# High and low halves of the stationary rows stored side by side in the output projection and layer 1

## The chip, the cores and the metric

The kernel runs on one core of one Trainium2 chip, as one launch. The metric is device time in microseconds, from the first to the last of the kernel's work on that core. Two runs of the kernel before gave 1775.3 and 1775.44 us, median 1775.37 us.

## The reference, cut to what matters

A two-layer backbone in float32 works on 256 latent tokens and 256 context tokens of width 2048. Layer 0 projects both streams, runs neighbourhood attention and a bidirectional state-space scan beside each other, and joins their 4096 output channels in one projection. Layer 1 is a gated short convolution between two more projections.

```python
# layer 0, after attention (ya) and the scan (yb)
out = jnp.concatenate([ya, yb], axis=-1) @ w_out          # 256x4096 @ 4096x2048
x = x + gate * out
# layer 1
h = modulate(rms_norm(x, norm_g[1]), shift, scale)
p = h @ sc_w_in                                           # 256x2048 @ 2048x8192
bg, cg, hv, g = jnp.split(p, 4, axis=-1)
y = bg * dw_conv(cg * hv, conv_w)
x = x + gate1 * ((jax.nn.silu(g) * y) @ sc_w_out)         # 256x2048 @ 2048x2048
```

## The kernel before, in words

**Products in three parts.** Each float32 operand of a large product is split into a high half, rounded to the matmul's fast float32 form (`F32R`), and a low half, the remainder. A product is then three matmuls: high times high, high times low, low times high. Weights come by DMA in pieces of 512 KB (`raw`), ScalarE writes their high half (`wH`, line 417) and VectorE their low half (`wL`, line 424). The activations are split once, where they are produced.

**Who is stationary.** `mm_act` keeps the activations stationary: for each block `kb` of 128 channels and each half `t` of the 256 tokens it loads 128 columns of the activation's high or low half into the array, and streams 512 columns of the weights through it. `mm_ws` does it the other way round, with weights stationary and 256 or 512 token columns moving. All of the output projection and of layer 1 goes through the first form, or through loops written out with the same three calls. So there the pair of halves of one activation block, a tile of 128 partitions by 2 by 256 elements, is read only as a stationary operand. Each matmul has its own weight load; the trace lists them apart, as PE (the matmul) and PEld (the load of its stationary operand). The calls all stand in one helper, line 192.

**Where the pairs of halves are made.** Four places write such a tile, always the high half on ScalarE and then the low half on VectorE: `put_mix` (line 945) and `mix_gen` (line 1562) for the 32 blocks of the output projection, `high` and `low` in `norm_gen` for the 16 blocks that enter layer 1, and `bg_gen` for the 16 blocks that enter its last projection. In the trace these tiles are named `mix`, `h` and `y`. They reuse the memory of the 32 tiles `hH0` to `hH15` and `hL0` to `hL15` of layer 0: `mix0` to `mix15` and `y` use the `hH` ones, `mix16` to `mix31` and `h` the `hL` ones. In layer 0 itself those tiles hold one half for 512 tokens each, and are read both as stationary and as moving operands.

**What sets the order.** The program is written out in one order by a planner inside the kernel. `Plan` keeps an estimated clock per engine and, per 128-element stretch of a tile, when it was last written and read; `pump` starts queued pieces of work (generators in `urgent`, `side` and `back`) between matmuls when the estimate says their inputs are ready. Three pools of scratch tiles (`tmp`, `half`, `raw`) are handed out by the same clocks, and a generator starts only when its share of `tmp` and `half` is free (`budget`). So a change in tile sizes or in a pool can move pieces of work in the order, without adding any.

Of the kernel before, what the change touches and what calls it, by code (L numbers as in the profile page):

```python
# [9 lines left out]
F32R = mybir.dt.float32r  # L10
# [21 lines left out]
for _name, _w in (("ident", 128), ("sel", 2), ("mhalf", 32), ("strip", 384), ("mask", 64)):  # L32
    _coff[_name] = (_n, _n + _w)
    _n += _w
NCONST, CFIRST = _n, 162


class Plan:
# [103 lines left out]
def kernel(ctx: ExitStack, tc, x, cx, ada0, w0, ada_w, ada_b, w_in, w_out, sc_in, sc_out, rpb, small, const,  # L142
# [3 lines left out]
    sb = ctx.enter_context(tc.tile_pool(name="sb", bufs=1))  # L146
# [6 lines left out]
    E = plan.add  # L153

    def st(shape, tag, dt=F32, name=None):
        return sb.tile(list(shape), dt, tag=tag, name=name or tag, bufs=1)

    def drt(shape, name):
        return dr.tile(list(shape), F32, name="dram_" + name)


    NTMP, NHALF, NRAW, NW = 9, 9, 5, 3
    free_t = [st([128, 512], f"tmp{k}") for k in range(NTMP)]
    free_h = [st([128, 256], f"half{k}") for k in range(NHALF)]
    free_b = [pj.tile([128, 512], F32, tag=f"bank{k}", name=f"bank{k}", bufs=1) for k in range(8)]
    free_r = [st([128, 1024], f"raw{k}") for k in range(NRAW)]
    WH = [st([128, 1024], f"wH{k}", F32R) for k in range(NW)]
    WL = [st([128, 1024], f"wL{k}", F32R) for k in range(NW)]
# [167 lines left out]
    def give(pool, *bs):  # L336
        pool.extend(bs)
# [300 lines left out]
    hH, hL = [None] * KB, [None] * KB  # L638
# [301 lines left out]
    def put_mix(i, o):  # L940
        if free_rows[0] > i % 16:

            yield W_("ACT", o)
            hl = st([128, 2, 256], f"hH{i}" if i < 16 else f"hL{i - 16}", F32R, name=f"mix{i}")
            E(S.copy(hl[:, 0], o))
            yield W_("DVE", hl[:, 0])
            E(V.tensor_tensor(out=hl[:, 1], in0=o, in1=hl[:, 0].bitcast(F32), op=ALU.subtract))
            mH[i] = hl
            give(free_h, o)
            return  # L950
        yield W_("AQ", o)
        E(DMA2.dma_start(mixd[i], o))
        give(free_h, o)
        written.add(i)
# [79 lines left out]
    def head_gen(a, h):  # L1034
# [89 lines left out]
        give(free_b, po)  # L1124
        attn[0] += 2
        yield from put_mix(hd, o)


# [242 lines left out]
    def group_gen(s, gi):  # L1371
# [104 lines left out]
        for b in range(2):  # L1476
            yield from put_mix(16 + 2 * g + b, ys[b])
# [70 lines left out]
    def mix_gen(ip):  # L1548
        pair = (2 * ip, 2 * ip + 1)
        yield when(lambda: all(i in written or mH[i] is not None for i in pair) and free_rows[0] > (2 * ip + 1) % 16)  # L1550
        pair = [i for i in pair if mH[i] is None]
        if not pair:
            return
        i0, n = pair[0], len(pair)
        yield W_("AQ", mixd[i0:i0 + n])
        mx = tmp()
        m3 = two(mx)
        E(DMA2.dma_start(m3[:, :n], mixd[i0:i0 + n].rearrange("b p c -> p b c")))
        yield W_("ACT", mx)
        for j, i in enumerate(pair):  # L1560
            hl = st([128, 2, 256], f"hH{i}" if i < 16 else f"hL{i - 16}", F32R, name=f"mix{i}")
            E(S.copy(hl[:, 0], m3[:, j]))
            E(V.tensor_tensor(out=hl[:, 1], in0=m3[:, j], in1=hl[:, 0].bitcast(F32), op=ALU.subtract))
            mH[i] = hl
        give(free_t, mx)

    def mixes(k):
        for ip in order[k::3]:
            yield from mix_gen(ip)
# [80 lines left out]
    def norm_gen():  # L1650
# [5 lines left out]
        hls = {}  # L1656
# [42 lines left out]

        def high(kb, tt):  # L1700
            if kb not in hls:
                hls[kb] = st([128, 2, 256], f"hL{kb}", F32R, name=f"h1_{kb}")
                h1[kb] = (hls[kb][:, 0], hls[kb][:, 1])
            E(S.activation(hls[kb][:, 0, tt], late[kb][:, tt], AF.Identity, bias=S1[:, kb:kb + 1], scale=1.0))

        def scaled(kb, tt):

            o = pts[kb // 4][:, kb % 4:kb % 4 + 2, tt]
            E(V.tensor_tensor(out=o, in0=o, in1=rb[0][:, tt].unsqueeze(1).to_broadcast([128, 2, 128]), op=ALU.mult))
            high(kb, tt)  # L1710
            high(kb + 1, tt)

        def pair(kp):
            yield when(lambda: ("turn", kp + 1) in got)
            yield W_("DVE", r2, held[kp] if kp in held else late[kp])
            for kb in (kp, kp + 1):
                if kb not in held:
                    E(V.tensor_tensor(out=late[kb], in0=late[kb], in1=r2, op=ALU.mult))
                else:
                    E(V.scalar_tensor_tensor(out=late[kb], in0=held[kb][:, (kb % 2) * 256:(kb % 2) * 256 + 256],  # L1720
                                             scalar=A1[:, kb:kb + 1], in1=r2, op0=ALU.mult, op1=ALU.mult))
                high(kb, slice(0, 256))
            if kp in held:
                give(free_b, held[kp])
            ahead()
# [52 lines left out]
    for ns in ((0, 512), (1024,), (1536,)):  # L1778
        pss = [banks(2) for n in ns]
        for ip in range(16):  # L1780
# [8 lines left out]
            if hold[0]:  # L1789
# [10 lines left out]
                for t in range(2):  # L1800
                    done_ = 0
                    for q, (H, Lo) in enumerate(ws):
                        for b in range(2):
                            i = 2 * order[NTAIL + q] + b
# [39 lines left out]
    v = st([128, 4, 256], "Btm", name="v")  # L1844
# [16 lines left out]
    def over(rows_, b):  # L1861

        yield W_("PE", *rows_, nb=1)
        pt = bank()
        for k in range(2):
            for t in range(2):
                turn(pt[:, k * 256 + t * 128:k * 256 + (t + 1) * 128], rows_[t][:, (b + k) * 128:(b + k + 1) * 128])
        return pt
# [39 lines left out]
    def bg_gen(i, ps):  # L1908
        for t in range(2):
            yield W_("DVE", ps[t])  # L1910
            E(V.tensor_tensor(out=sg[t], in0=ps[t], in1=sg[t], op=ALU.mult))
            give(free_b, ps[t])
        for b in range(0, 4, 2):
            pt = yield from over(sg, b)
            yield W_("DVE", pt)
            E(V.tensor_tensor(out=flat(v[:, b:b + 2, :]), in0=pt, in1=flat(v[:, b:b + 2, :]), op=ALU.mult))
            give(free_b, pt)
            yield W_("ACT", v[:, b:b + 2, :])
            for k in range(2):
                kb = 4 * i + b + k  # L1920
                hl = st([128, 2, 256], f"hH{kb}", F32R, name=f"y2_{kb}")
                E(S.copy(hl[:, 0], v[:, b + k, :]))
                yield W_("DVE", hl[:, 0])
                E(V.tensor_tensor(out=hl[:, 1], in0=v[:, b + k, :], in1=hl[:, 0].bitcast(F32), op=ALU.subtract))
                y2[kb] = hl

    for i in range(4):
        for part, gen in ((1, cg_gen), (2, hv_gen), (3, gg_gen), (0, bg_gen)):
            ps = banks(2)
            kb0 = 0  # L1930
            if i == 0 and part == 1:

                kb0 = 8
                ws = []
                for t in range(2):
                    for kb in range(8):
                        force(lambda: ("h1", kb, t) in got, (urgent,))
                        if kb // 2 == len(ws):
                            ws.append(use(kb // 2))
                        H, Lo = ws[kb // 2]  # L1940
                        tt = slice(t * 128, (t + 1) * 128)
                        for a_, w_ in ((0, H), (0, Lo), (1, H)):
                            mm(ps[t], h1[kb][a_][:, tt], w_[:, kb % 2], kb == 0 and a_ == 0 and w_ is H, False)
                        if t and kb % 2:
                            used()
                        pump()
            for kb in range(kb0, KB, 2):
                force(lambda: ("h1", kb + 1, 1) in got)
                chunk(kb, "act", ps, kb == 0, kb == KB - 2, lambda i: h1[i])
            spawn(urgent, ordered(4 * i + (1, 2, 3, 0).index(part), gen(i, ps)), 2 if i == 0 and part in (1, 2) else 0)  # L1950
# [30 lines left out]
    for t in range(2):  # L1981
        for q, (H, Lo) in enumerate(ws):
            for b in range(2):
                hl = y2[KB - 6 + 2 * q + b]
# [66 lines left out]
```

## Time and profile before

| what | us |
|---|---|
| two runs | 1775.3 and 1775.44 |
| the profiled execution, first to last instruction | 1770.0 |
| TensorE matmuls, busy | 1749.4 |
| weight loads, busy (they overlap matmuls) | 1472.7 |
| VectorE busy | 1262.5 |
| ScalarE busy | 773.7 |
| output projection, first to last matmul start | 1127.4 to 1318.7 |
| matmuls of layer 1's first projection | 1319.8 to 1677.1 |
| matmuls of layer 1's last projection | 1677.4 to 1765.1 |

A group in the profile is named by what it writes and reads: `bank<-wH,mix` is a matmul that streams `wH` past the stationary `mix` into a PSUM bank, and the load with the same name loads that stationary. In the timeline the columns are start, length, engine, line, operation, tiles, shape and count; lengths of matmuls overlap, because the next one starts before the last has drained, so the pace is read from one start to the next. In the table by windows each engine has its busy time and its number of instructions in brackets.

### The profile page before, as it was taken

Reading aid. Unit: us, or ns where it says so; the run is one execution under the profiler, and the core shown is the slowest. Engines: PE = TensorE matmul, PEld = TensorE weight load, DVE = VectorE, ACT = ScalarE, POOL = GpSimd, SP = SyncE. Lnnn points to the kernel's source line nnn. Section 1 sums busy time; section 2 is a strip of 40 time slices with the busy share of each in tenths; the row PEclk is TensorE's granted clock in tenths of the full one; section 3 lists DMA queues with packets and bytes.
Section 4 is the critical chain, followed back from the end, with each engine's and each line's share of the span. In section 5 each row is a group of like instructions: output and inputs, shape, how many; then the busy total and the mean of one; then the engine's idle time right before and its main releaser. Section 6 shows DMA issues by size and latency. Waiting matters only on the chain.

```text
span 1770.0 us, 25382 instructions
## 1 busy us (share of the span) xinstructions
PE 1749.4 (99%) x9577; PEld 1472.7 (83%) x9577; DVE 1262.5 (71%) x1986; ACT 773.7 (44%) x1330; POOL 31.3 (2%) x28
## 2 busy tenths in 40 slices
PE   6999999999999999999999999999999999999998
PEld 4777988888888889888888898888888888888887
DVE  5656788878686878775878777786668777555554
ACT  5423544455242445342445343564546344444442
POOL 0000100001000001000001000000000000000000
PEclk9999999999999999999999999999999999999999
DMA  9977644666746666655666556658867787666563
GB/s 362 348 284 255 208 148 142 194 203 202 232 140 200 200 195 200 207 148 185 205 191 191 160 174 213 189 184 286 284 224 242 250 259 253 207 188 190 190 211 119
DMA packets 218138, 374.60 MB, mean 212 GB/s; under 512 B 32304, under 2 KB 69008, under 8 KB 218016
## 3 DMA queue, kind: packets, MB, share of 16 engines
q1 hardware_dynamic: 210704, 366.38, 64.1%
q10 hardware_dynamic: 7312, 6.61, 1.2%
q8 instruction: 75, 1.23, 0.3%
q14 instruction: 47, 0.39, 0.1%
HBM read 367.52 MB, written 6.72 MB: 211 GB/s over the span
## 4 chain that ended last, share of the span: by engine, by line
PE 97%; DMA 1%; DVE 1%; ACT 0%; SPq 0%; issue 0%; POOL 0%; DVEq 0%; ACTq 0%
PE bank L192 94%; PE bank L196 3%; DMA tmp<-dram_csr 1%; DMA raw<-in_ada 0%; DVE wL L424 0%; DVE acc L812 0%; SPq L578 0%; DVE tmp L1405 0%; DVE tmp L1416 0%; DVE tmp L598 0%; ACT wH L417 0%; DVE acc L798 0%; DVE half L1443 0%; ACT tmp L1401 0%; ACT half L719 0%
## 5 line engine op out<-in xcount | busy, mean ns | idle before, releaser
L417 ACT CAST wH<-raw 128x1024 fp32r<-128x1024 f32 (+1 forms) x375 | 392.0, 1046 | 586.1 <-PE bank L192 493.1
L424 DVE TENSOR_TENSOR wL<-raw,wH 128x1024 fp32r<-128x1024 f32 (+1 forms) x374 | 453.4, 1215 | 219.5 <-ACT wH L417 217.9
L192 PE MATMUL bank<-hH,wH 128*128 128x256 f32 (+1 forms) x1040 | 342.9, 330 | 0.0
L192 PE MATMUL bank<-hL,wH 128*128 128x256 f32 (+1 forms) x1040 | 336.8, 324 | 0.0
L192 PE MATMUL bank<-hH,wL 128*128 128x256 f32 (+1 forms) x1024 | 331.1, 323 | 0.0
L192 PE MATMUL bank<-wH,hH 128*128 128x512 f32 x640 | 256.4, 401 | 2.6 <-ACT hH L752 2.6
L192 PE MATMUL bank<-wL,hH 128*128 128x512 f32 x640 | 250.1, 391 | 0.0
L192 PE MATMUL bank<-wH,hL 128*128 128x512 f32 x640 | 249.8, 391 | 0.1
L812 DVE SCALAR_TENSOR_TENSOR acc<-raw,csil,acc 128x512 f32<-128x512 f32 x256 | 191.7, 749 | 62.3 <-DMA raw<-in_ada_w 55.6
L192 PE MATMUL bank<-wH,h 128*128 128x512 f32 x680 | 215.7, 391 | 0.0
L192 PEld LDWEIGHTS bank<-hH,wH 128*128 128x128 f32 x1040 | 197.7, 190 | 17.0 <-issue 2.2
L192 PEld LDWEIGHTS bank<-hL,wH 128*128 128x128 f32 x1040 | 197.9, 190 | 15.0
L192 PEld LDWEIGHTS bank<-hH,wL 128*128 128x128 f32 x1024 | 194.6, 190 | 15.7 <-DVE wL L424 0.4
L192 PEld LDWEIGHTS bank<-wH,h 128*128 128x128 f32 x680 | 127.6, 188 | 26.6 <-issue 0.2
L192 PEld LDWEIGHTS bank<-wH,hH 128*128 128x128 f32 x640 | 120.6, 189 | 30.6 <-issue 4.6
L192 PEld LDWEIGHTS bank<-wH,hL 128*128 128x128 f32 x640 | 120.4, 188 | 25.5 <-DVE hL L758 0.6
L192 PEld LDWEIGHTS bank<-wL,hH 128*128 128x128 f32 x640 | 120.7, 189 | 23.9 <-DVE wL L440 0.3
L192 PE MATMUL bank<-wH,mix 128*128 128x512 f32 x432 | 137.9, 392 | 0.0
L192 PE MATMUL bank<-wL,h 128*128 128x512 f32 x340 | 132.3, 389 | 0.0
L192 PEld LDWEIGHTS bank<-wH,mix 128*128 128x128 f32 x432 | 81.1, 188 | 16.7 <-issue 0.2
L192 PE MATMUL bank<-wL,mix 128*128 128x512 f32 x216 | 84.1, 389 | 0.0
L192 PEld LDWEIGHTS bank<-wL,h 128*128 128x128 f32 x340 | 63.9, 188 | 12.9
(284 smaller groups left out, 2168.2 us busy)
## 6 DMA issues: line engine op xcount, KB each, us to landing
raw<-in_w_in SPq DMA_DIRECT2D x196, 512.0 KB, 3.9
raw<-in_ada_w SPq DMA_DIRECT2D x128, 512.0 KB, 4.7
raw<-in_sc_in SPq DMA_DIRECT2D x128, 512.0 KB, 3.7
raw<-in_w_out SPq DMA_DIRECT2D x64, 512.0 KB, 4.9
raw<-in_ada SPq DMA_DIRECT2D x36, 512.0 KB, 5.9
raw<-in_sc_out SPq DMA_DIRECT2D x32, 512.0 KB, 4.1
PT<-in_ada SPq DMA_DIRECT2D x16, 512.0 KB, 8.9
tmp<-dram_csr SPq DMA_DIRECT2D x32, 256.0 KB, 6.4
```

The source lines that it names most:

```text
L192: E(T.matmul(o, l, r, start=start, stop=stop, skip_group_check=True))
L196: E(T.transpose(o, i, ident if k == 128 else ident[:k, :k]))
L417: E(S.copy(H, v))
L424: E(V.tensor_tensor(out=Lo, in0=v, in1=H.bitcast(F32), op=ALU.subtract))
L812: E(V.scalar_tensor_tensor(out=acc, in0=v[:, j], scalar=csil[:, 2 * k + j:2 * k + j + 1], in1=acc, op0=ALU.mult, op1=ALU.add))
```

## The change

The tile of 128 by 2 by 256 elements stays as large, but element `c` of the high half now stands at place `2c` and element `c` of the low half at `2c + 1`. A half is then read and written with a step of two elements (8 bytes), where it was contiguous. This holds for `mix`, `h` and `y`. Layer 0's own use of the tiles is contiguous as before.

Besides, the tiles `hL0` to `hL3` grow from 512 to 576 elements, and the pairs stored in them begin 8, 16, 32 and 48 elements (32, 64, 128 and 192 bytes) further on. That concerns `mix16` to `mix19` and `h` blocks 0 to 3. The 1 KB per partition for it comes from the pool `half`, which has eight tiles and not nine.

```diff
+SHIFT = {"hL0": 8, "hL1": 16, "hL2": 32, "hL3": 48}

     def st(shape, tag, dt=F32, name=None):
+        if tag in SHIFT:
+            return sb.tile([128, 576], dt, tag=tag, name=name or tag, bufs=1)[:, :512]
         return sb.tile(list(shape), dt, tag=tag, name=name or tag, bufs=1)
+
+    def pair_rows(tag, name):
+
+        wide = tag in SHIFT
+        v = sb.tile([128, 576 if wide else 512], F32R, tag=tag, name=name, bufs=1)
+        o = SHIFT.get(tag, 0)
+        return v[:, o:o + 512].rearrange("p (c a) -> p a c", a=2)

-    NTMP, NHALF, NRAW, NW = 9, 9, 5, 3
+    NTMP, NHALF, NRAW, NW = 9, 8, 5, 3
...
-            hl = st([128, 2, 256], f"hH{i}" if i < 16 else f"hL{i - 16}", F32R, name=f"mix{i}")
+            hl = pair_rows(f"hH{i}" if i < 16 else f"hL{i - 16}", f"mix{i}")
             E(S.copy(hl[:, 0], o))
             yield W_("DVE", hl[:, 0])
             E(V.tensor_tensor(out=hl[:, 1], in0=o, in1=hl[:, 0].bitcast(F32), op=ALU.subtract))
...
-                hls[kb] = st([128, 2, 256], f"hL{kb}", F32R, name=f"h1_{kb}")
+                hls[kb] = pair_rows(f"hL{kb}", f"h1_{kb}")
...
-                hl = st([128, 2, 256], f"hH{kb}", F32R, name=f"y2_{kb}")
+                hl = pair_rows(f"hH{kb}", f"y2_{kb}")
```

`mix_gen` changes in the same way as `put_mix`.

More of the change, by code (lines that the diff above doesn't have):

```diff
@@ L1560, in mix_gen @@
         for j, i in enumerate(pair):
-            hl = st([128, 2, 256], f"hH{i}" if i < 16 else f"hL{i - 16}", F32R, name=f"mix{i}")
+            hl = pair_rows(f"hH{i}" if i < 16 else f"hL{i - 16}", f"mix{i}")
             E(S.copy(hl[:, 0], m3[:, j]))
```

## The prediction

> **What bounds the kernel now.** I read the page first, then the table by windows over the stages that the change touches, then the timeline for the pace of single matmuls.
>
> ```profile
> span 1770.0 us, 25382 instructions
> ...
> PE 1749.4 (99%) x9577; PEld 1472.7 (83%) x9577; DVE 1262.5 (71%) x1986; ACT 773.7 (44%) x1330; POOL 31.3 (2%) x28
> ...
> PEclk9999999999999999999999999999999999999999
> ...
> PE 97%; DMA 1%; DVE 1%; ACT 0%; SPq 0%; issue 0%; POOL 0%; DVEq 0%; ACTq 0%
> ```
>
> TensorE is the chain: 97% of what ended last, at a full clock in every slice. So a microsecond is won or lost only by the pace of the matmuls, or by a wait in front of them. The stages of the change, by windows: end of layer 0, output projection, the seam between the layers, layer 1's two projections.
>
> ```profile
> core 0: us, PE busy (x) PEld busy (x) DVE busy (x) ACT busy (x) POOL busy (x), PEclk, DMA share, GB/s
> 1080.00:1127.00 47.00, 47.00 (x232) 38.65 (x232) 27.34 (x56) 19.95 (x43) 0.00 (x0) 1.00 0.62 189
> 1127.00:1315.00 188.00, 188.00 (x903) 156.44 (x902) 137.92 (x202) 97.16 (x149) 1.39 (x2) 1.00 0.73 247
> 1315.00:1320.00 5.00, 5.00 (x28) 4.19 (x27) 3.19 (x10) 2.73 (x7) 0.56 (x1) 1.00 0.58 212
> 1320.00:1677.00 357.00, 356.99 (x1633) 294.91 (x1632) 235.21 (x286) 162.62 (x199) 0.94 (x1) 1.00 0.68 219
> 1677.00:1770.00 93.00, 88.50 (x395) 72.96 (x393) 47.61 (x52) 29.69 (x31) 0.00 (x0) 0.99 0.50 165
> ```
>
> Up to 1677 TensorE never stops; in the last stage it stops for 4.5 us. VectorE is busy for 137.92 of 188 us and 235.21 of 357 us, ScalarE for less. The instructions that touch the three rearranged tiles, with the whole span as window, in the order `mix`, `h`, `y` (columns: PE, PEld, DVE, ACT):
>
> ```profile
> 0.00:1770.00 1770.00, 178.79 (x768) 143.05 (x768) 12.17 (x32) 11.47 (x32) 1.00 0.66 212
> 0.00:1770.00 1770.00, 352.37 (x1536) 287.23 (x1536) 8.41 (x24) 8.86 (x24) 1.00 0.66 212
> 0.00:1770.00 1770.00, 87.75 (x384) 71.92 (x384) 6.21 (x16) 5.88 (x16) 1.00 0.66 212
> ```
>
> That is 768 + 1536 + 384 = 2688 matmuls whose stationary operand is now read with a step, all 512 columns wide. **One nanosecond more or less for each of them is 2.69 us.**
>
> **The pace of a matmul, and what is fixed in it.** Starts in the timeline: first 512 columns in layer 1, then 256 columns in layer 0, then attention's products with the halves of V, also 256 columns.
>
> ```profile
> 1559.71 1.75 PE L192 MATMUL bank<-KL,h 128*128 128x512 f32 x7
> 1561.30 0.39 PE L192 MATMUL bank<-QT,h 128*128 128x512 f32 x1
> ```
>
> ```profile
> 205.75 0.28 PE L192 MATMUL bank<-hH,wH 128*128 128x256 f32 x1
> ...
> 207.55 0.28 PE L192 MATMUL bank<-hH,wH 128*128 128x256 f32 x1
> ```
>
> ```profile
> 278.04 0.28 PE L192 MATMUL bank<-PH,VH 128*128 128x256 f32 x1
> ...
> 279.44 0.40 PE L192 MATMUL bank<-KT,QT 128*128 128x512 f32 x1
> ```
>
> Seven starts in 1.59 us are 227 ns each (over long steady stretches of the trace, 226.7); fifteen in 1.80 us are 120.0; twelve in 1.40 us are 116.7. From 256 to 512 columns the pace grows by 106.7 ns, 0.417 ns a column. So 226.7 − 512 × 0.417 = 13.3 ns are left that do not depend on the width. This rest comes once with each load of 128 stationary columns. It is not merely a price of swapping operands: V's halves lie 32 bytes off the 512-byte raster on which the program's addresses place all other operands of these matmuls, and with them the rest is 116.7 − 106.7 = 10.0 ns. So where the stationary lies in memory changes the rest, and I read it as time that the moving stream loses while the stationary is fetched.
>
> **The change part by part.** *The load itself.* It has room, as its length, its start and a narrower load show:
>
> ```profile
> L192 PEld LDWEIGHTS bank<-wH,h 128*128 128x128 f32 x680 | 127.6, 188 | 26.6 <-issue 0.2
> ...
> L192 PEld LDWEIGHTS bank<-tmp,xtm 128*64 128x64 f32 x128 | 7.2, 136 | 4.2 <-issue 1.8 <-DVE tmp L1421 1.6 <-DVE tmp L1416 0.7
> ```
>
> ```profile
> 1500.16 0.19 PEld L192 LDWEIGHTS bank<-wL,h 128*128 128x128 f32 x1
> 1500.38 0.39 PE L192 MATMUL bank<-wL,h 128*128 128x512 f32 x1
> ```
>
> ```profile
> 206.23 0.19 PEld L192 LDWEIGHTS bank<-hH,wL 128*128 128x128 f32 x1
> ...
> 206.35 0.28 PE L192 MATMUL bank<-hH,wL 128*128 128x256 f32 x1
> ```
>
> From 64 to 128 columns a load grows by 52 ns, so of the 188 ns some 104 scale with the columns. In layer 1 its matmul starts 220 ns after it, some 30 ns after its end; in layer 0, 120 ns after it, before its end. A load whose scaling part doubled would let its matmul go at 120 + 104 = 224 ns, still inside 226.7: nothing. If the matmul waited for the longer load's end and the same 30 to 36 ns after it, it would start at 188 + 104 + 36 = 328 ns: 101 ns × 2688 = +272 us. I take the lower end, since layer 0 shows matmuls that do not wait for the end.
>
> *The rest of 13.3 ns.* No row shows a stationary with a step. A load now spans 1024 bytes of each partition instead of 512. Lower bound: all of the rest goes, −13.3 × 2688 = −35.8 us; nearest row below, V's 10.0 ns: −9 us. Upper bound: it is paid per stretch of memory fetched, of which there are twice as many: +13.3 ns, a pace of 240, +35.8 us. I take the upper end: the one row that moves the rest at all ties it to where the stationary is fetched, and twice as much memory is walked through in the same load.
>
> [...]
>
> *The four shifted tiles.* `mix16` to `mix19` serve 4 × 24 matmuls and `h` 0 to 3 serve 4 × 96: 480 of the 2688. By V's row a 32-byte offset is worth −3.3 ns, −1.6 us if all four had it; with the opposite sign +1.6. I take 0.
>
> *Writing with a step.* VectorE writes the low halves in 12.17 + 8.41 + 6.21 = 26.8 us, ScalarE the high ones in 11.47 + 8.86 + 5.88 = 26.2 us. No row shows such a write. Unchanged is one bound (a gain is excluded, a scattered write is no less work), doubled the other: +27 us on each engine. TensorE covers it, since both engines have over a quarter of each stage free. Where that cover is thin is the seam: the first blocks of `h` are awaited there, and 8 of the 24 half-block pairs in a row at 8.41 / 24 + 8.86 / 24 = 0.72 us, less their overlap, could add up to 3 us. I take 1 us.
>
> *The order.* The program built from the change has exactly the same instructions; 52 of 1237 places differ on ScalarE, 88 of 1988 on VectorE and 34 of 833 on SyncE, nearly all around the output projection, because of the smaller pool and the planner's wider stretches. The two windows up to 1315 have TensorE busy for 235 of 235 us, so work moved between matmuls only trades places. 0, with ±2 us.
>
> Sum: 1770.0 + 35.8 + 1 = 1806.8 us for the profiled span; the 5.4 us by which the median of the runs (1775.37) exceeds this span stay. **Forecast: 1812 us**, 2.1% slower; its own range is 1790 (half of the step is paid) to 1850 (the load's doubling shows as well).
>
> **Rivals.** *Nothing happens* (1776 us): the load is hidden by its slack and the rest stays 13.3 ns. For it: 226.7 and 120.0 are 17 and 9 times 13.3, as if starts were held to a raster, where a small extra cost vanishes. Against it: V's 116.7 is on no such raster.
>
> *Faster: the two streams stop disturbing each other.* The moving operand passes 4 bytes per 0.417 ns; a contiguous load of 104 ns passes 512 bytes, half as fast, so the streams drift past each other all through it. With a step of 8 bytes the load passes 1024 bytes in 104 ns, as fast as the moving one. Streams in step can miss each other for good. If half of the rest goes, the time is 1775.4 − 17.9 = 1757 us, at V's rest 1766, at most 1740. For it: V's row says that relative position matters. Against it: nothing in the trace shows the rest below 10 ns at full streaming pace. It decides if the pace of `h` falls below 226 ns.
>
> *The load becomes the bound*: up to 1775 + 272 = 2047 us, if the stepped load takes over 300 ns. Against it is the slack above.
>
> **How the numbers follow.** Forecast 0.42, nothing 0.24, faster 0.20, load the bound 0.14. The range of 8 in 10 goes from 1755 (most of faster) to 1870 (forecast with a partly longer load) and leaves out the far end of the load and the last of faster. Two per cent, about what a measurement of this kernel can tell from no change, is 35.5 us, so slower begins at 1811 and faster below 1740. Slower has all of the load's case and about 0.3 of the forecast's, 0.45; faster has the extreme of its rival, 0.03; the rest, 0.52, is within.
>
> **What would show it.** The pace of `bank<-wH,h` in the timeline decides: near 240 ns the forecast, 227 nothing, 213 to 223 faster, far over 240 the load, whose length (188 ns now) would then show it. The pace at blocks 0 to 3 of `h` beside the other blocks shows what the shift does. Layer 0 must stay at 227 and 120 ns; if the time moves there, or TensorE stops between 1315 and 1320, my sum has left out a wait.

## The result, and the profile after

| | us | ratio to the kernel before, 95% interval |
|---|---|---|
| before, median of 2 runs | 1775.37 | |
| after, median of 2 runs (1790.53 and 1792.55) | 1791.54 | 1.0097 [1.008, 1.0114] |

The change makes the kernel slower by 16.2 us, 0.97%. The forecast was 1812 us: the direction is right, the size is more than twice too large. The page of the changed kernel:

```profile
span 1788.4 us, 25384 instructions
...
PE 1766.5 (99%) x9577; PEld 1488.8 (83%) x9577; DVE 1263.4 (71%) x1986; ACT 773.1 (43%) x1330; POOL 32.2 (2%) x28
...
PE 95%; DMA 2%; DVE 2%; ACT 1%; issue 0%; SPq 0%; POOL 0%; DVEq 0%; ACTq 0%
```

The span grew by 18.4 us and TensorE's busy time by 17.1 us, with the same 9577 matmuls. VectorE and ScalarE are as busy as they were. TensorE is still the chain, with 95% of what ended last, so the time should have gone into the pace of matmuls. Where, the table by windows tells for the instructions that touch the three rearranged tiles, in the order `mix`, `h`, `y` (columns: PE, PEld, DVE, ACT):

```profile
0.00:1788.40 1788.40, 184.00 (x768) 147.52 (x768) 12.27 (x32) 12.01 (x32) 1.00 0.65 209
0.00:1788.40 1788.40, 361.47 (x1536) 296.26 (x1536) 8.42 (x24) 9.03 (x24) 1.00 0.65 209
0.00:1788.40 1788.40, 91.10 (x384) 75.30 (x384) 6.31 (x16) 6.26 (x16) 1.00 0.65 209
```

Against before, TensorE is busy for 5.21, 9.10 and 3.35 us more: 17.66 us together, nearly all that the span gained. The pace is read best where one moving tile is used twelve times in a row: from the start of that row to the start of the next are twelve matmuls. The timeline of before, and then of after, in layer 1's first projection:

```profile
1340.18 2.88 PE L192 MATMUL bank<-KL,h 128*128 128x512 f32 x12
1342.90 0.39 PE L192 MATMUL bank<-QT,h 128*128 128x512 f32 x1
```

```profile
1570.51 2.96 PE L203 MATMUL bank<-KL,h 128*128 128x512 f32 x12
1573.31 0.39 PE L203 MATMUL bank<-QT,h 128*128 128x512 f32 x1
...
1741.36 2.99 PE L203 MATMUL bank<-KL,y 128*128 128x512 f32 x12
1744.19 0.40 PE L203 MATMUL bank<-QT,y 128*128 128x512 f32 x1
```

Before, 2.72 us for twelve, 226.7 ns each. After, 2.80 us, 233.3 ns each, and 2.83 us, 235.8 ns, at `y`. So a matmul with a stepped stationary costs 6.67 ns more, not 13.3. Layer 0 has kept its pace; fourteen starts in 1.68 us are still 120.0 ns:

```profile
205.32 0.28 PE L203 MATMUL bank<-hH,wH 128*128 128x256 f32 x1
...
207.00 0.28 PE L203 MATMUL bank<-hH,wL 128*128 128x256 f32 x1
```

The groups of single tiles (minimum, median and maximum of the length in ns, then first and last start) show the load after, and the writes of ScalarE and VectorE, first contiguous (before, lines 1562 and 1563) and then stepped (after):

```profile
L203 PEld LDWEIGHTS bank<-wH,h x680: 192/193/198, 1325.7 to 1689.2; 128*128 128x128 f32 x170
```

```profile
L1562 ACT CAST mix<-tmp x24: 390/402/408, 1095.1 to 1137.0; 128x256 fp32r<-128x256 f32 x24
L1563 DVE TENSOR_TENSOR mix<-tmp,mix x24: 416/418/427, 1096.9 to 1138.6; 128x256 fp32r<-128x256 f32 x24
...
L1573 ACT CAST mix<-tmp x24: 399/418/427, 1096.0 to 1138.2; 128x256 fp32r<-128x256 f32 x24
L1574 DVE TENSOR_TENSOR mix<-tmp,mix x24: 416/418/429, 1097.9 to 1140.1; 128x256 fp32r<-128x256 f32 x24
```

The load takes 193 ns where it took 188. ScalarE's write took 402 ns before and takes 418; VectorE's is 418 ns in both.

### The profile page after: what moved, and what is told of

Same layout as the page of the kernel before. It is cut to its first block, busy times and chain, and to the rows that moved or that the text cites. A ratio compares the mean times of both kernels' runs of the same rounds, so it can differ in the third digit from the quotient of the medians.

```text
span 1788.4 us, 25384 instructions
## 1 busy us (share of the span) xinstructions
PE 1766.5 (99%) x9577; PEld 1488.8 (83%) x9577; DVE 1263.4 (71%) x1986; ACT 773.1 (43%) x1330; POOL 32.2 (2%) x28
## 4 chain that ended last, share of the span: by engine, by line
PE 95%; DMA 2%; DVE 2%; ACT 1%; issue 0%; SPq 0%; POOL 0%; DVEq 0%; ACTq 0%
PE bank L203 92%; PE bank L207 3%; DMA tmp<-dram_csr 1%; DMA raw<-in_ada 0%; DVE wL L435 0%; DVE acc L823 0%; ACT wH L428 0%; DVE tmp L1416 0%; DVE tmp L1427 0%; ACT tmp L1412 0%; SPq L589 0%; DVE half L1454 0%; DVE half L1451 0%; DVE tmp L609 0%; ACT tmp L1422 0%
## 5 line engine op out<-in xcount | busy, mean ns | idle before, releaser
L203 PE MATMUL bank<-wH,h 128*128 128x512 f32 x680 | 219.5, 395 | 0.0
L203 PEld LDWEIGHTS bank<-hH,wH 128*128 128x128 f32 x1040 | 197.8, 190 | 17.1 <-issue 2.2
L203 PEld LDWEIGHTS bank<-wH,h 128*128 128x128 f32 x680 | 131.7, 194 | 26.7 <-issue 0.4
```

The source lines that it names most:

```text
L203: E(T.matmul(o, l, r, start=start, stop=stop, skip_group_check=True))
```

## The experiments

Twelve runs, all beside runs of the kernel before on the same chip (its median 1772.69 to 1774.26 us). Single profiles of the same instructions differ by some 3 us in when layer 0 ends; the stretch from the first matmul on `mix` to the first on `y`, 550.0 us before and 564.1 us after, does not share that.

**1. The step alone.** The tiles are not enlarged or shifted and the pool `half` keeps nine tiles; the rest is the change.

```diff
-SHIFT = {"hL0": 8, "hL1": 16, "hL2": 32, "hL3": 48}
+SHIFT = {}
-    NTMP, NHALF, NRAW, NW = 9, 8, 5, 3
+    NTMP, NHALF, NRAW, NW = 9, 9, 5, 3
```

> The halves side by side, without the shift of four tiles and with all nine tiles of the pool half; TensorE's order is that of the kernel before. If the step of the stationary read is the cause, the pace of the 2688 matmuls is 233.3 ns everywhere, blocks 0 to 3 included, against 226.7 before: +6.67 x 2688 = +17.9 us, 1793 us, some 1 us more than the changed kernel, whose shifted blocks run at 229 to 234 ns. If the shift or the moved order is the cause, it is 1775 to 1777 us.

Measured: 1792.48 us, ratio 1.01 [1.0085, 1.0115]. The step by itself makes the whole loss. Its windows for `mix`, `h` and `y`:

```profile
0.00:1789.40 1789.40, 183.49 (x768) 147.31 (x768) 12.20 (x32) 11.85 (x32) 1.00 0.66 209
0.00:1789.40 1789.40, 362.15 (x1536) 295.77 (x1536) 8.46 (x24) 9.04 (x24) 1.00 0.66 209
0.00:1789.40 1789.40, 90.23 (x384) 73.98 (x384) 6.24 (x16) 6.11 (x16) 1.00 0.66 209
```

Against before, TensorE has 9.78 us more on `h` and 2.48 us more on `y`, which is 6.4 and 6.5 ns for each matmul. `y` does not show the 3.35 us of the changed kernel; the last run below comes back to that.

**2. The shift, the pool and the order alone.** Contiguous halves as before, but `hL0` to `hL3` enlarged and shifted, and `half` with eight tiles.

```diff
-        return v[:, o:o + 512].rearrange("p (c a) -> p a c", a=2)
+        return v[:, o:o + 512].rearrange("p (a c) -> p a c", a=2)
```

> The halves contiguous again, but the shift of four tiles, the smaller pool and so nearly the order of the changed kernel kept. If the step is the cause, the pace is 226.7 ns but for the 480 matmuls on shifted blocks, which may go to 223 to 235: 1773 to 1778 us. If the order or the pool costs the time, it is 1790 us.

Measured: 1777.16 us, ratio 1.002 [1.0011, 1.003]. Windows for `mix`, `h` and `y`:

```profile
0.00:1777.80 1777.80, 179.92 (x768) 143.02 (x768) 12.26 (x32) 11.58 (x32) 1.00 0.67 211
0.00:1777.80 1777.80, 354.59 (x1536) 287.37 (x1536) 8.41 (x24) 8.88 (x24) 1.00 0.67 211
0.00:1777.80 1777.80, 87.76 (x384) 71.95 (x384) 6.31 (x16) 5.97 (x16) 1.00 0.67 211
```

TensorE has 1.13 and 2.22 us more than before on `mix` and `h`, and only 96 and 384 of their matmuls read shifted pairs. On `h` that is 5.8 ns for each. The 1.13 us on `mix` would be 11.8 ns for each, so part of it has another source, the order for instance; this was not separated. From the first matmul on `mix` to the first on `y` it is 553.3 us, 3.3 more than before. So a contiguous stationary that merely lies elsewhere also costs nearly the 6.67 ns, with no more memory walked through. That spoke against the price per stretch of memory, and the next runs pursue it.

Not every other place costs something. The enlarged tiles push block 1 of `mix` and block 1 of `y`, 24 matmuls each, 256 bytes out of the old relation to the weights, by the program's addresses. Yet `y` takes 87.76 us where it took 87.75; 24 times 6.67 ns would be 0.16 us.

**3. Twice the step.** The low and high halves of both token halves interleaved, so that a half is read with a step of 16 bytes and a load walks through 2048 bytes. The writes step by 16 bytes as well. As in the first experiment no tile is shifted. One line of the edit:

```diff
+        self.v = v.rearrange("p (c t a) -> p a t c", t=2, a=2)
```

> Each stationary half read with a step of four elements (16 bytes): the halves of both token halves share one stretch, element c of half a of tokens t at place 4c + 2t + a. If the loss grows with the memory that a load walks through (512 bytes 13.3 ns, 1024 bytes 20.0 ns), 2048 bytes give 33.3 ns or more, a pace of 246.7: +20 x 2688 = +54 us, 1829 us. If any step other than one costs the same single stretch of 6.67 ns, it is 1793 us. [...]

Measured: 1808.78 us, ratio 1.0193 [1.0178, 1.0208]. The load and the pace:

```profile
L225 PEld LDWEIGHTS bank<-wH,h x680: 307/310/334, 1331.0 to 1705.5; 128*128 128x128 f32 x170
```

```profile
1358.55 2.98 PE L225 MATMUL bank<-KL,h 128*128 128x512 f32 x12
1361.37 0.39 PE L225 MATMUL bank<-QT,h 128*128 128x512 f32 x1
```

Now the load is long, 310 ns, and still the pace is 2.82 us for twelve, 235 ns: four times the memory of before, and 8.3 ns more. In a steady row, neither a price in proportion to the memory walked (226.7 + 3 × 6.67 = 246.7 ns, if the step of two elements set the scale) nor a load that bounds the pace (310 ns and more) is what happens. The matmul does go before its load has ended: the first load with `KL` starts at 1332.4 us and its matmul at 1332.6, while such a load takes 0.31 us.

The run as a whole loses more than this pace explains: 8.3 ns for 2688 matmuls are 22.3 us, and it takes 34.8 us longer than before. Twice TensorE stops and waits for weights, 4.9 us in all, and after each stop the granted clock (PEclk, the last column but two) is about half, 0.55 over 3.4 us and 0.50 over 2.4 us:

```profile
1132.00:1135.40 3.40, 3.26 (x8) 2.61 (x9) 3.40 (x8) 3.40 (x9) 0.00 (x0) 0.55 0.74 217
1355.00:1357.40 2.40, 2.40 (x7) 1.91 (x6) 2.40 (x3) 0.91 (x1) 0.00 (x0) 0.50 0.71 215
```

So the total of this run is not to be read as a price of the step; why TensorE has to wait there was not followed up.

**4 and 5. Contiguous halves, 32 or 64 bytes off the weights.** The kernel before with 8 or 16 elements of padding ahead of the tiles of layer 0's activations. Weights stay where they were, and the tiles of the activations (with `mix`, `h` and `y`) move against them. The order of the instructions is that of before on every engine. With 64 bytes one small scratch tile also shares the memory of another.

```diff
+    st([128, 8], "pad")
     xnT = [st([128, 512], ("Bl", "Cl")[kb] if kb < 2 else f"hL{kb}", name=f"xm{kb}") for kb in range(KB)]
```

> The kernel before with 32 unused bytes in front of the activation tiles, so that all stationary rows lie 32 bytes off the place that the moving weights have in a 512-byte raster, in layer 0 too; the order on every engine is that of the kernel before. If the relative place sets the loss as with V's halves before (10.0 ns, not 13.3), the pace of 4608 matmuls of 512 columns and 1920 of 256 falls by 3.3 ns: up to -22 us, 1754 us. If only the step matters, it is 1775 us. If the 235 ns seen at the one start before V's products is what a 32-byte offset costs behind 512 columns, it is +8 x 4608 = +38 us, 1813 us.

> The kernel before, contiguous rows, all activation tiles 64 bytes off. If the fetch repeats every 64 bytes, this is aligned again: 226.7 ns, 1775 us. If it repeats in a wider raster, some 233 ns for 512 columns, 1800 us; any pace below 226.7 ns would make this the fastest version.

Measured: 1799.96 us with 32 bytes, ratio 1.0149 [1.0132, 1.0166], and 1799.54 us with 64 bytes (one run). This is slower than the change itself, without any step, because layer 0's wide matmuls pay as well (by the record of starts 233.2 ns on average with 32 bytes, 227.6 before); `h` alone takes 362.04 us of TensorE with 32 bytes and 362.14 with 64, as in run 1 with the step (362.15). The timeline with 32 bytes, in layer 0, in attention's products with V and in layer 1:

```profile
205.30 0.28 PE L192 MATMUL bank<-hH,wL 128*128 128x256 f32 x1
...
206.94 0.28 PE L192 MATMUL bank<-hL,wH 128*128 128x256 f32 x1
...
280.21 0.28 PE L192 MATMUL bank<-PL,VH 128*128 128x256 f32 x1
...
281.53 0.40 PE L192 MATMUL bank<-KT,QT 128*128 128x512 f32 x1
...
1354.88 2.96 PE L192 MATMUL bank<-KL,h 128*128 128x512 f32 x12
1357.68 0.40 PE L192 MATMUL bank<-QT,h 128*128 128x512 f32 x1
```

With 512 columns 2.80 us for twelve, 233.3 ns, the pace of the changed kernel. With 256 columns fourteen starts in 1.64 us, 117.1 ns, which is less than the 120.0 of before. So the row of attention's products with V on which the prediction leaned (256 columns, 32 bytes off, 116.7 ns) is confirmed, but its sign turns round at 512 columns. V itself shows the same from the other side: by the program's addresses this padding cancels its 32 bytes, and its products go at 120.0 ns here (eleven starts in 1.32 us), where they went at 116.7.

**6 and 7. Step and offset together.** The first experiment with the same padding of 32 and 64 bytes, one run each.

> Side by side, and all activation tiles 32 bytes off the raster of the moving weights (layer 0, contiguous, too). For the 2688 stepped matmuls: if the loss is set by how much memory a load walks through, the pace is 233.3 ns as without the offset. If it is set by where the two streams stand to each other, it changes, to the 229 to 231 ns that the short runs on the block shifted by 32 bytes had in the changed kernel, or lower. The rest of the kernel is as in the run of contiguous rows 32 bytes off (233.3 ns for 512 columns, 118.6 for 256): some 1800 us if the stepped ones stay at 233, 1788 at 229.

> The same with 64 bytes. By memory walked through 233.3 ns for the stepped matmuls; by place 230 to 236, as the short runs on the block shifted by 64 bytes had. Contiguous rows of layer 0: 226.7 if the raster is of 64 bytes, 233 if it is wider.

Measured: 1797.25 and 1789.60 us. The stepped matmuls with 64 bytes:

```profile
1351.44 2.92 PE L203 MATMUL bank<-KL,h 128*128 128x512 f32 x12
1354.20 0.39 PE L203 MATMUL bank<-QT,h 128*128 128x512 f32 x1
```

2.76 us for twelve, 230.0 ns. With 32 bytes TensorE has 14.11 us more than before on the three tiles, 5.2 ns for each matmul, so that the pace lies between the two values expected. The two prices do not add up: with 64 bytes of offset a stepped stationary is faster (230.0) than a contiguous one (233.3, run 5) and faster than a stepped one without offset (233.3).

**8. Fewer places.** The kernel before, with other reads of the stationary in layer 1: in its first projection all 128 columns are the same element (no memory is walked through), in its last the step is three elements. Both projections then multiply with other activations than the reference's.

```diff
+        if name.startswith("y2_"):
+            l = bass.AP(tensor=l.tensor, offset=l.offset // 128, ap=[[512, 128], [3, 128]])
+        elif name.startswith("h1_"):
+            l = l[:, :1].to_broadcast([128, 128])
```

> The kernel before, but what the stationary operand reads is changed and with it the result: in layer 1's first projection all 128 columns read one and the same place (4 bytes per partition), in its last projection they read the tile with a step of three elements (12 bytes). If the loss is proportional to the memory walked through, the first projection's pace falls to 213 ns (-13 x 1536 = -20 us for that stage). If the 13.3 ns are a fixed raster of two stretches of 6.67 ns, it stays at 226.7, or loses one stretch, 220. [...]

Measured: 1784.02 us (one run). The window of `h`, then the pace in both projections and the loads:

```profile
0.00:1782.10 1782.10, 358.16 (x1536) 288.17 (x1536) 8.39 (x24) 8.87 (x24) 1.00 0.65 210
```

```profile
1342.91 2.91 PE L197 MATMUL bank<-KL,h 128*128 128x512 f32 x12
1345.66 0.40 PE L197 MATMUL bank<-QT,h 128*128 128x512 f32 x1
...
1701.11 2.99 PE L197 MATMUL bank<-KL,y 128*128 128x512 f32 x12
1703.94 0.39 PE L197 MATMUL bank<-QT,y 128*128 128x512 f32 x1
```

```profile
L197 PEld LDWEIGHTS bank<-wH,h x680: 185/188/192, 1322.4 to 1682.8; 128*128 128x128 f32 x170
...
L197 PEld LDWEIGHTS bank<-wH,y x168: 251/252/254, 1689.1 to 1777.0; 128*128 128x128 f32 x168
```

Reading a single element takes 2.75 us for twelve, 229 ns, and over the whole stage 358.16 us against 352.37, which is 3.8 ns more for each matmul. That is slower than the contiguous 226.7, where a price per memory walked should have given about 213. Unless reading one place over and over has a cost of its own, this rules out the forecast's reason. With the step of three elements it is 2.83 us for twelve, 235.8 ns, and a load takes 252 ns.

**9 and 10. Read or write.** Both halves of the change are separated on the 1152 matmuls of `mix` and `y`. Run 9 is the kernel before, which writes contiguously, with a stepped read; run 10 is the first experiment, which writes with a step, with a contiguous read. The edit of the helper that issues the matmuls is shown first for run 9, then for run 10. In both, the output projection and the last projection multiply with high and low halves mixed up. `h` keeps the read of the kernel that each starts from.

```diff
+        if l.tensor.name.startswith(("mix", "y2_")):
+            l = bass.AP(tensor=l.tensor, offset=l.offset // 256 + l.offset % 256 // 128 * 256, ap=[[512, 128], [2, 128]])
```

```diff
+        if l.tensor.name.startswith(("mix", "y2_")):
+            l = bass.AP(tensor=l.tensor, offset=l.offset % 2 * 256 + l.offset // 256 * 128, ap=[[512, 128], [1, 128]])
```

> The kernel before, with contiguous rows, but the matmuls of the output projection and of layer 1's last projection (tiles mix and y2, 768 + 384 = 1152 matmuls) read 128 elements with a step of 8 bytes out of the same tile; the stationary rows are then a mixture of high and low halves, so the result is not the reference's. If the step of the read is the whole cause: 233.3 ns at mix and y, 226.7 at h, 1152 x 6.67 = +7.7 us, about 1783. If the writing with a step or the changed tiles take part in it: less, down to 1775 and 226.7 ns everywhere.

> The experiment with the halves side by side in whole 512-byte tiles, but the same 1152 matmuls (tiles mix and y2) read 128 contiguous elements out of the side-by-side rows; the writes keep their step, and the result is not the reference's. If the read is the whole cause: 226.7 ns at mix and y, 233.3 at h, about 1792 - 7.7 = 1785. If writing with a step slows TensorE's reads: 233.3 ns everywhere, 1792.

Measured: 1781.54 us, ratio 1.0048 [1.0031, 1.0065], and 1784.29 us, ratio 1.006 [1.0045, 1.0075]. Windows for `mix`, `h` and `y`, of run 9 and then of run 10:

```profile
0.00:1777.70 1777.70, 183.49 (x768) 147.31 (x768) 12.17 (x32) 11.45 (x32) 1.00 0.65 211
0.00:1777.70 1777.70, 352.37 (x1536) 287.27 (x1536) 8.41 (x24) 8.87 (x24) 1.00 0.65 211
0.00:1777.70 1777.70, 91.10 (x384) 75.30 (x384) 6.21 (x16) 5.89 (x16) 1.00 0.65 211
```

```profile
0.00:1781.30 1781.30, 178.79 (x768) 143.08 (x768) 12.21 (x32) 11.81 (x32) 1.00 0.65 210
0.00:1781.30 1781.30, 362.20 (x1536) 295.57 (x1536) 8.44 (x24) 9.05 (x24) 1.00 0.65 210
0.00:1781.30 1781.30, 87.75 (x384) 71.92 (x384) 6.22 (x16) 6.14 (x16) 1.00 0.65 210
```

TensorE's times follow the read alone. With a stepped read `mix` takes 183.49 us, as in the first experiment, though written contiguously. With a contiguous read it takes 178.79 us, to the hundredth what it took before, though written with a step. ScalarE's times follow the write (11.81 against 11.45 us on `mix`), and nobody waits for that.

**11. Everything moved together.** The kernel before, with the 32 bytes of padding ahead of all tiles, so that weights and activations keep their relation.

```diff
+    st([128, 8], "pad")
     free_t = [st([128, 512], f"tmp{k}") for k in range(NTMP)]
```

> The kernel before, with every tile of the memory moved by the same 32 bytes, so that stationary and moving operand keep their relation to each other and only the place of both changes. If the relation decides: 226.7 and 120 ns and 1775, no change. If the place decides, as an alignment of each operand by itself: about 233 ns wherever 512 columns are moved, 1797 to 1800 as with half of the tiles moved, or more, as now both operands are off.

Measured: 1776.33 us, ratio 1.0011 [0.9998, 1.0023].

```profile
1560.74 2.88 PE L193 MATMUL bank<-KL,h 128*128 128x512 f32 x12
1563.46 0.39 PE L193 MATMUL bank<-QT,h 128*128 128x512 f32 x1
```

2.72 us for twelve, 226.7 ns again, and 550.0 us from `mix` to `y`, as before. By the program's addresses nearly all operands of these matmuls lie 128 bytes past a multiple of 512 before, and 160 bytes past it here. So, for contiguous rows, it is not the place of the stationary by itself that costs the 6.67 ns, but its relation to the place of the moving one: 226.7 ns with both moved by 32 bytes, 233.3 with the stationary moved alone (run 4).

**12. The changed kernel again.**

> The changed kernel once more. If the 235 to 239 ns at the last projection's high halves belong to this order of instructions and these places, they come again, and the time is 1790 to 1793; if they were of one execution, y runs at 233.3 ns there too.

Measured: 1790.98 us, and `y` takes 91.10 us of TensorE again, as in run 9, which has another order of instructions around it. So it was no chance of one execution. By the record of starts, the three kinds of matmul on `y` take 235.0, 238.3 and 233.3 ns in these runs and 233 to 234 ns in the first experiment, with the same steps and, but for one block, the same places modulo 512 bytes. Run 1 was on another chip than runs 9 and 12, so the chip is not excluded. Why a stage settles in the one pattern or the other stays open; it is worth 0.9 us.

## Why the prediction was wrong, and where it was right

**What bounds the kernel** was right: TensorE stays the chain, and 17.66 us of slower matmuls account for the 18.4 us of the span.

**The load itself, zero from a span of 0 to 272 us**: right. It takes 193 ns instead of 188, and its matmul does not wait for its end; run 3 shows even a load of 310 ns under a pace of 235. Nor are the 5 ns more of load the 6.67 ns: run 4's loads are no longer than before, 287.49 against 287.23 us on `h`, and its matmuls are as slow as the stepped ones (233.3 ns). The load's length by the step was 188 ns for contiguous rows or one element, 193 for step two, 252 for step three and 310 for step four. The pace of the matmuls does not follow it: with a step of two the load is only 5 ns longer and the matmul behind it loses 6.67 ns, and from step two to step four the load grows by 117 ns and the pace by 1.7.

**The rest of 13.3 ns doubles, +35.8 us**: this is the step that failed. The rest went from 13.3 to 20.0 ns, so it grew by half of what was forecast: 17.66 us were measured over the 2688 matmuls. The reason, "it is paid per stretch of memory fetched", was wrong, and not only its size: no memory walked through leaves 229.2 − 213.3 = 15.9 ns by run 8's twelve, 512 bytes leave 13.3 or 20.0 according to where they lie (runs 4 and 11), 1024 bytes 20.0 or 16.7 (runs 1 and 7), 2048 bytes 21.7 (run 3). The sign came out as forecast, but not for the reason given, and that much was luck.

What the runs show in its place: at 512 columns, contiguous rows in the same relation to the weights as before, or 256 bytes from it (run 2), have the least rest seen; every other offset or step that was tried costs 2.5 to 9 ns more. That a step of two elements costs this because it gives up that relation, as an offset does, is a reading: the two prices are alike (runs 1 and 4) and do not add up (runs 6 and 7), but no run shows how the one becomes the other. That it is the moving stream that loses the time while the stationary is fetched also fits and was not shown. The prediction had one row that moved the rest at all, V's, at another width; it took from it that the relative place matters, which runs 4 and 11 bear out, and then a scale, which it could not give.

**The four shifted tiles, 0 ± 1.6 us**: wrong in size when alone (+3.3 us in run 2, and 5.8 ns for each shifted matmul on `h`, where V's row had suggested 3.3 either way). In the changed kernel no loss by them can be seen: 1791.54 us, against 1792.48 without them in run 1.

**Stepped writes, hidden but for 1 us**: right in that they are hidden. ScalarE's cost 16 ns more of 402, VectorE's nothing, and run 10's `mix` and `y` run as before with them. The 1 us at the seam was not needed. Windows of after over the seam and the stage behind it:

```profile
1320.00:1326.00 6.00, 5.83 (x30) 4.62 (x30) 4.25 (x11) 2.73 (x7) 0.56 (x1) 1.00 0.47 154
1326.00:1692.00 366.00, 366.00 (x1633) 303.91 (x1632) 234.77 (x284) 162.35 (x199) 0.94 (x1) 1.00 0.66 213
```

TensorE stops for 0.17 us there, and then not until layer 1's last projection.

**The order, 0 ± 2 us**: nothing can be seen of it. After 564.1 us and the first experiment 564.5 us from `mix` to `y` differ in order and shift, by 0.4 us.

**The rivals.** "Nothing happens" rested on a raster of 13.3 ns, and 233.3 is on no such raster. The paces 226.7, 233.3 and 120.0 are 34, 35 and 18 times 6.67, but the 116.7, 230.0 and 235 ns of other rows are no multiples of that either, so no raster is shown. "Two streams in step miss each other" was right in that the relation of the two streams counts, but it asked for a pace below 226 ns, and no run came near it at 512 columns, with 64 bytes of offset (230.0) either. "The load becomes the bound" fell with runs 3 and 8.

## What to carry to other kernels

Here TensorE was the chain and the loads of 188 ns hid under matmuls of 226.7 ns, and still the way the stationary lay moved the pace, to 233.3 ns. So read the start-to-start time of a long row of equal matmuls, and after any change of layout or any padding look whether it has moved by a few ns, since that multiplies by thousands (6.67 ns by 2688 matmuls are 17.9 us). In this kernel 32 bytes of padding ahead of the activations cost each wide matmul as much as the strided read did (233.3 ns in both), and moving all tiles together cost nothing (226.7 ns), so it is worth trying to keep stationary and moving operands in the relation that the fast stage has. And one row that shows an effect at another width proves that there is an effect; its size and even its sign have to be measured where they are wanted: 32 bytes took 2.9 ns off at 256 columns (120.0 to 117.1 ns) and added 6.67 at 512.

## What the runs showed of the hardware

Moving the tiles of the activations by 32 bytes against those of the weights slowed this kernel by 1.49% [1.32, 1.66], about as much for each wide matmul as the step did (233.3 ns in both, where it was 226.7); moving all of them by the same 32 bytes changed nothing to speak of (1.0011 [0.9998, 1.0023]). The length of the load hardly showed in the pace of the matmuls (188 to 310 ns of load for a pace of 227 to 236). The place of what it reads did: the same contiguous load of 188 ns went with 226.7 ns before and with 233.3 in run 4, according to its place beside the moving operand. Why the one relation is the better one was not found. The narrower matmuls go the other way: 256 columns take 117.1 ns with the 32 bytes and 120.0 without. A kernel that shifted only the operands of layer 0's narrow matmuls, and kept the wide ones, was not tried.
